# A fused attention, DeltaNet and RG-LRU layer: the order of work at the seams of its stages, and the engine of some elementwise steps

## The chip, the cores and the metric

The kernel runs on one core of one Trainium2 chip. The metric is the device time of one execution in microseconds (us). Times before: 1758.59, 1755.84 and 1751.17, median 1755.84.

## What is computed

One layer, on x of 2048 tokens by 1024 channels in float32:

```python
h = rmsnorm(x, norm_w)
u = h @ W_in                        # 1024 x 5128, split into column groups
a_q,a_k,a_v,a_z, g_q,g_k,g_v,g_z, g_b,g_a, r_x,r_z = split(u)
y_a = diff_attention(a_q, a_k, a_v, lam, subln_w) * silu(a_z)   # 4 heads, block-causal, chunk 64
y_g = gated_deltanet(...)           # causal conv of width 4 on q, k, v; chunked WY form; * silu(g_z)
y_r = rg_lru(...) * silu(r_z)       # causal conv of width 4, gates, linear scan over positions
x = x + concat(y_a, y_g, y_r) @ W_out                           # 1536 x 1024
out = rmsnorm(x, final_norm_w)
```

In diff_attention each head has two softmax maps; the second is subtracted with weight lam. The result is normalised per head.

## The kernel before

Every float32 product is made of three matmuls: each operand is split into a rounded high part and a low remainder (high by ACT, remainder by DVE), and PE adds high x high, low x high and high x low. So each weight group and each activation goes through a split before PE can use it.

**Projection stage, 0 to about 1143 us.** The tokens are taken in two halves of 1024 (hf), each of two blocks of 512 (sb). A half has 40 jobs; a job is one group of 128 columns of W_in, or, for the values, half of the 1024 contraction rows of 256 columns (`values`, two jobs that go together). `unit` (L286) does a job for one block with 24 matmuls of 128x512; `unit_v` (L297) does the values. The list `order` (L352) says which job and block come next. `half_jobs` (L1316) makes the list of jobs: the values of the first two heads, then for each GDN head its key, query, value and gate groups with four or five of the other groups (attention az, aq, ak; LRU rx, rz) between them, then what is left of the others, and last the values of the other two heads.

Weights are fetched and split by `next_w` (L1380): it waits two steps, splits the group that was fetched, and asks for the next one. At most two jobs' weights are live (`refill`, L1374); their tiles have the tag wx, of which there are five. Work that is not a matmul of a job runs in generators in the list bgs, which are advanced by `pump` between matmuls: norms and transposes of the next x block (`norm_x` L211, `next_hT` L265), the convolutions (`conv`, L349: first tap on POOL at L351, three more on DVE at L355), the triangular solve of the GDN (L576 to L649), its chain over chunks (`Gdn.main`, L674 to L709) and output (`Gdn.out`, scaling at L731), the LRU (gates L769, scan L808 and L809), and the splitting of W_out (`split_wo`, L864). The x block 2 is loaded near the end of the first half and transposed from job 39 on; block 3 is loaded after the last unit of the half.

**Attention and output projection, 1143 us to the end.** `all_scores` (L1170) yields the scores of one block of 128 queries against up to 512 keys at a time: two matmuls (L1036, L1037) into a bank with the tag tp (three bufs), a maximum on DVE (L1040), an exponential on ACT (L1048). `turn` (L1103) transposes the probabilities on PE (L1111), with evacuations on ACT (L1118) and DVE (L1120), and `apply` multiplies by the values (L1128 to L1130). `norm_sq` and `norm_out` (L1145) make the sums for the norm with two matmuls, L1148 and L1149, into the tile ss, with the tag pj (two bufs). Queries, keys, values and gates of 512 tokens come back from memory by `fetch_kv` (L996); it is called one step before it is needed. Between these, `out_stream` (L904) supplies matmuls of the output projection (L893 to L895) as filling, into the tag pj; its operands come by `load_wo` (L872, tiles lt, big, g) and `fetch_y` (L879 high, L880 low). For head 3 its result is added to the sum so far at L966, also a reader of pj.

A scheduler lays the instructions of the program on the queues of the engines and may place them earlier or later than the program has them, within their dependences; every engine then runs its own queue in order. All loads and stores go through SP's queue.

```python
pss = psum.tile([P, 256], F32, name="ss", tag="pj", bufs=2)                # L1147
...
bgs.append(next_w(2))                                                      # L1378
```

## Time and profile before

| | |
|---|---|
| times | 1758.59, 1755.84, 1751.17 us, median 1755.84 |
| the profiled execution: time, span | 1750.52 us, 1748.8 us |
| mean granted clock of PE | 0.996 |
| PE busy | 1697.3 us (97%), 9494 matmuls |
| DVE busy | 1286.4 us (74%) |
| ACT busy | 1005.7 us (58%) |
| POOL busy | 305.3 us (17%) |
| DMA | 261.65 MB, mean 150 GB/s |

The profiled execution ran 5.3 us under the median. Times inside it are counted from the start of its span. Busy PE means that a matmul is under way; its idle time is span less busy, 51.5 us. The granted clock is 1.0 at full speed.

### The profile page before, as it was taken

Reading aid. Unit: us, or ns where it says so; the run is one execution under the profiler, and the core shown is the slowest. Engines: PE = TensorE matmul, PEld = TensorE weight load, DVE = VectorE, ACT = ScalarE, POOL = GpSimd, SP = SyncE. Lnnn points to the kernel's source line nnn. Section 1 sums busy time; section 2 is a strip of 40 time slices with the busy share of each in tenths; the row PEclk is TensorE's granted clock in tenths of the full one; section 3 lists DMA queues with packets and bytes.
Section 4 is the critical chain, followed back from the end, with each engine's and each line's share of the span. In section 5 each row is a group of like instructions: output and inputs, shape, how many; then the busy total and the mean of one; then the engine's idle time right before and its main releaser. Section 6 shows DMA issues by size and latency. Waiting matters only on the chain.

```text
span 1748.8 us, 27889 instructions
## 1 busy us (share of the span) xinstructions
PE 1697.3 (97%) x9494; PEld 1414.3 (81%) x9494; DVE 1286.4 (74%) x3043; ACT 1005.7 (58%) x2568; POOL 305.3 (17%) x458
## 2 busy tenths in 40 slices
PE   7999999999999899999999999999999999999998
PEld 6887777887879888787887887977888888887786
DVE  5576786686686567678778678578787777778896
ACT  6634534535435554453553534368778878877684
POOL 3011200201101111131221210011213213211011
PEclk9999999999999999999999999999999999999999
DMA  6233242242244434435445424697797898596432
GB/s 182 68 91 94 60 121 76 82 108 68 88 121 146 145 85 133 136 115 168 137 135 173 123 88 142 185 285 197 194 245 205 273 233 232 159 285 209 162 132 103
DMA packets 309298, 261.65 MB, mean 150 GB/s; under 512 B 67082, under 2 KB 242468, under 8 KB 309156
## 3 DMA queue, kind: packets, MB, share of 16 engines
q1 hardware_dynamic: 309156, 259.87, 50.9%
q8 instruction: 75, 1.23, 0.3%
q14 instruction: 67, 0.55, 0.1%
HBM read 175.88 MB, written 83.92 MB: 149 GB/s over the span
## 4 chain that ended last, share of the span: by engine, by line
PE 61%; DVE 10%; issue 7%; DMA 4%; ACT 3%; POOL 2%; SPq 1%; POOLq 0%; DVEq 0%; ACTq 0%
PE pj L290 10%; PE pj L291 10%; PE pj L292 10%; PE pj L895 3%; PE pj L893 3%; PE pj L894 3%; PE s L1036 2%; PE s L1037 2%; PE pt L1111 2%; DVE s L355 2%; DVE tt L589 1%; DVE tt L595 1%; DMA wx<-xo_sp 1%; PE tp L542 1%; PE av L1130 1%
## 5 line engine op out<-in xcount | busy, mean ns | idle before, releaser
L290 PE MATMUL pj<-hp,wx 128*128 128x512 f32 x1120 | 461.4, 412 | 2.4 <-DVE s L367 2.4
L292 PE MATMUL pj<-hp,wx 128*128 128x512 f32 x1120 | 444.5, 397 | 0.0
L291 PE MATMUL pj<-hp,wx 128*128 128x512 f32 x1120 | 444.1, 397 | 0.0
L292 PEld LDWEIGHTS pj<-hp,wx 128*128 128x128 f32 x1120 | 210.5, 188 | 47.9
L290 PEld LDWEIGHTS pj<-hp,wx 128*128 128x128 f32 x1120 | 211.0, 188 | 45.3 <-DVE s L367 2.9
L291 PEld LDWEIGHTS pj<-hp,wx 128*128 128x128 f32 x1120 | 211.5, 189 | 41.9
L1040 DVE TENSOR_REDUCE nm<-s 128x1 f32<-128x512 f32 (+3 forms) x320 | 191.7, 605 | 28.3 <-PE s L1037 25.1
L1048 ACT ACTIVATE s<-s,nm 128x512 f32<-128x512 f32 (+3 forms) x272 | 170.8, 629 | 52.3 <-DVE nm L1040 51.4
L355 DVE SCALAR_TENSOR_TENSOR s<-raw,pcol,s 128x512 f32<-128x512 f32 x192 | 143.8, 749 | 41.7 <-POOL s L351 38.8
L279 ACT ACTIVATE wx<-wx 128x1024 fp32r<-128x1024 f32 (+1 forms) x76 | 80.5, 1059 | 88.5 <-PE pj L291 82.4
L1036 PE MATMUL s<-hp 128*128 128x512 f32 (+3 forms) x320 | 124.8, 390 | 5.0 <-ACT s L1048 3.8
L283 DVE TENSOR_TENSOR wx<-wx 128x1024 fp32r<-128x1024 f32 (+1 forms) x77 | 94.2, 1224 | 45.6 <-ACT wx L279 43.7
L1037 PE MATMUL s<-hp 128*128 128x512 f32 (+3 forms) x320 | 118.0, 369 | 0.0
L1111 PE MATMUL pt<-ident,s 128*128 128x128 f32 x544 | 86.3, 274 | 4.0 <-DVE s L1099 3.9
L589 DVE TENSOR_TENSOR tt<-lt,tt 128x248 f32<-128x248 f32 (+30 forms) x248 | 82.2, 331 | 6.2
L893 PE MATMUL pj<-g,wx 128*128 128x512 f32 x208 | 85.4, 411 | 0.1
L1099 DVE SCALAR_TENSOR_TENSOR s<-s,cf,s 128x512 f32<-128x512 f32 (+2 forms) x112 | 75.1, 701 | 11.1 <-ACT s L1087 6.5
L346 POOL COPY halo<-raw 128x3 f32<-128x3 f32 x48 | 14.9, 311 | 386.2 <-ACT raw L344 375.0
L895 PE MATMUL pj<-g,wx 128*128 128x512 f32 x208 | 82.2, 395 | 0.0
L894 PE MATMUL pj<-g,wx 128*128 128x512 f32 x208 | 82.1, 395 | 0.0
L595 DVE TENSOR_TENSOR tt<-tt 128x248 f32<-128x248 f32 (+30 forms) x248 | 76.9, 310 | 6.6
L309 PE MATMUL pj<-wx,hp 128*128 128x264 f32 (+1 forms) x256 | 77.1, 302 | 4.4 <-ACT wx L279 1.9
(337 smaller groups left out, 3849.6 us busy)
## 6 DMA issues: line engine op xcount, KB each, us to landing
wx<-in_w_in_dram SPq DMA_DIRECT2D x78, 512.0 KB, 4.2
wx<-y_sp SPq DMA_DIRECT2D x64, 512.0 KB, 6.5
hp<-k_sp SPq DMA_DIRECT2D x64, 256.0 KB, 6.5
wo_sp<-s SPq DMA_DIRECT2D x48, 256.0 KB, 2.3
v_sp<-s SPq DMA_DIRECT2D x64, 128.0 KB, 3.2
q_sp<-s SPq DMA_DIRECT2D x32, 256.0 KB, 2.3
k_sp<-s SPq DMA_DIRECT2D x32, 256.0 KB, 2.6
y_sp<-go SPq DMA_DIRECT2D x32, 256.0 KB, 2.7
```

What stands on the lines that cost most here:

```text
L290: nc.tensor.matmul(ps, wh[:, kt, :], hb[kt][:, 0, :], start=(kt == 0), stop=False)
L291: nc.tensor.matmul(ps, wh[:, kt, :], hb[kt][:, 1, :], start=False, stop=False)
L292: nc.tensor.matmul(ps, wl[:, kt, :], hb[kt][:, 0, :], start=False, stop=(kt == KT - 1))
L355: nc.vector.scalar_tensor_tensor(y, raw[:, t : t + SB], pc(wcol(t)), y, op0=ALU.mult, op1=ALU.add)
L893: nc.tensor.matmul(ps, yh, wh, start=first, stop=False)
L894: nc.tensor.matmul(ps, yh, wl, start=False, stop=False)
L895: nc.tensor.matmul(ps, yl, wh, start=False, stop=last)
L1036: nc.tensor.matmul(ps[:, :n], qq, kh[:, :n], start=True, stop=False)
L1037: nc.tensor.matmul(ps[:, :n], qq, kl[:, :n], start=False, stop=True)
L1040: nc.vector.tensor_reduce(nm[:, u, m, kb : kb + 1], ps[:, :n], axis=AX.X, op=ALU.max, negate=True)
L1048: nc.scalar.activation(ee[:, :n], ps[:, :n], AF.Exp, bias=nm[:, u, m, kb : kb + 1], accum_out=zp[:, u, m, kb : kb + 1],)
L1111: nc.tensor.transpose(pt[:, off + (u - us[0]) * P : off + (u - us[0] + 1) * P], e[(u, kt // 4)][:, (kt % 4) * P : (kt % 4 + 1) * P], ident,)
```

## The change

- `norm_x`: the scalings of the x tiles of blocks 2 and 3 (8 in all) go from POOL to ACT.
- `conv`: the first of four taps (64 in all) goes from POOL to ACT.
- `Gdn.out`: the scaling of the outputs (64 of 128x128) goes from POOL to ACT.
- `split_wo`: the subtraction (24) goes from POOL to DVE.
- `norm_out`: for head 3, the tile ss has the tag tp instead of pj.
- `all_scores`: the first two blocks of queries, keys and values are fetched at once at the start, and the second is not fetched again.
- `next_half`, in place of two calls of `next_h`: x block 3 is loaded as soon as block 2 is transposed.
- The last five of the other groups come as rx, az, rz, aq, ak instead of az, rx, aq, ak, rz, and behind the second pair of value jobs, not ahead of it. Each half ends with aq and ak, block by block.
- The weights of the second value job of the second half are fetched one job ahead, into the tile lt. For two jobs of each half, `next_w` waits no steps instead of two.

```diff
--- before.py
+++ after.py
@@ -207,6 +207,10 @@
         for t, xx in enumerate(xt):
             if sb == 1 and t < 2:
                 nc.vector.tensor_scalar(xx, xx, rs[:, t : t + 1], None, op0=ALU.mult)
+            elif sb == 3 and t < 2:
+                nc.scalar.activation(xx, xx, AF.Copy, scale=rs[:, t : t + 1])
+            elif sb > 1:
+                nc.scalar.activation(xx, xx, AF.Copy, scale=rs[:, t : t + 1])
             else:
                 nc.gpsimd.tensor_scalar(
                     xx, xx, rs[:, t : t + 1], 0.0, op0=ALU.mult, op1=ALU.add
@@ -346,10 +350,10 @@
             nc.gpsimd.tensor_copy(halo[:, gi, :], raw[:, SB : SB + 3])
         return raw
 
-    def conv(raw, wcol, bias=0.0):
+    def conv(raw, wcol, bias=None):
         y = at([P, SB], "s16", 16)
-        nc.gpsimd.tensor_scalar(
-            y, raw[:, 3 : 3 + SB], pc(wcol(3)), bias, op0=ALU.mult, op1=ALU.add
+        nc.scalar.activation(
+            y, raw[:, 3 : 3 + SB], AF.Identity, scale=pc(wcol(3)), bias=zero if bias is None else bias
         )
         for t in range(3):
             nc.vector.scalar_tensor_tensor(
@@ -728,8 +732,8 @@
                 ro, ro, 1.0 / math.sqrt(P), rn[:, 1, sl], op0=ALU.mult, op1=ALU.mult
             )
             for c in range(4):
-                nc.gpsimd.tensor_scalar(
-                    os_[:, c, :], os_[:, c, :], ro[:, c : c + 1], 0.0, op0=ALU.mult, op1=ALU.add
+                nc.scalar.activation(
+                    os_[:, c, :], os_[:, c, :], AF.Copy, scale=ro[:, c : c + 1]
                 )
             yield from wait(7)
             pt = tp()
@@ -861,7 +865,7 @@
         wp = at([P, SB], "s16", 16, F32R)
         nc.scalar.activation(wp, wr, AF.Copy)
         wl = at([P, SB], "s16", 16, F32R)
-        nc.gpsimd.tensor_tensor(wl, wr, wp.bitcast(F32), op=ALU.subtract)
+        nc.vector.tensor_tensor(wl, wr, wp.bitcast(F32), op=ALU.subtract)
         yield from wait(6)
         nc.sync.dma_start(wo_sp[e, dh, :, 0, :], wp.bitcast(F32))
         nc.sync.dma_start(wo_sp[e, dh, :, 1, :], wl.bitcast(F32))
@@ -1144,7 +1148,7 @@
 
     def norm_out(h, i, oo):
         o2, t1, oh, ol = oo
-        pss = psum.tile([P, 256], F32, name="ss", tag="pj", bufs=2)
+        pss = psum.tile([P, 256], F32, name="ss", tag="pj" if h < 3 else "tp", bufs=2 if h < 3 else 3)
         nc.tensor.matmul(pss, onesr, oh, start=True, stop=False)
         nc.tensor.matmul(pss, onesr, ol, start=False, stop=True)
         nc.scalar.activation(o2, pss, AF.Ln, scale=1.0 / P, bias=epsA)
@@ -1171,10 +1175,11 @@
         for n, (h, i) in enumerate(steps):
             if n + 1 < len(steps):
                 h2, i2 = steps[n + 1]
-                if i2 % 2 == 0 and i2 > 0:
+                if i2 % 2 == 0 and i2 > 0 and i2 // 2 not in heads[h2].q:
                     fetch_kv(heads[h2], h2, i2 // 2)
             if n == 0:
-                fetch_kv(heads[0], 0, 0)
+                for kb in range(2):
+                    fetch_kv(heads[0], 0, kb)
                 yield
             for _ in scores(heads[h], h, i, es[n]):
                 yield
@@ -1276,9 +1281,15 @@
 
     bgs.append(start_h())
 
-    def next_h(n, xt):
-        yield from next_hT(hbs[n], xt)
-        ready[n] = True
+    def next_half(xt):
+        yield from next_hT(hbs[2], xt)
+        ready[2] = True
+        yield
+        xt = load_x(3)
+        while hbs[3] is None:
+            yield
+        yield from next_hT(hbs[3], xt)
+        ready[3] = True
 
     def params():
         pps = psum.tile([P, SB], F32, name="pps", tag="tp", bufs=3)
@@ -1327,6 +1338,9 @@
                 (partial(fetch_w, COL_RZ + h * P), None, r.outp),
             ]
 
+        az, rx, aq, ak, rz = others[-5:]
+        others[-5:] = [rx, az, rz, aq, ak]
+
         def values(pair):
             return [
                 (partial(fetch_v, pair, part, pair == 0), None, (gbs if pair == 0 else None, pair))
@@ -1344,7 +1358,7 @@
             ]
             for _ in range((4, 5, 5, 4)[h]):
                 jobs.append(others.pop(0))
-        return gbs, jobs + others + values(1)
+        return gbs, jobs + values(1) + others
 
     halves = [half_jobs(hf) for hf in range(2)]
     njob = len(halves[0][1])
@@ -1363,6 +1377,7 @@
                 order += [(a, 0), (a, 1), (a + 1, 0), (a + 1, 1)]
 
     nxt = Stage()
+    ahead = {}
     nxt.j, nxt.wr, nxt.live, nxt.busy = 4, jobs[4][0](), 2, False
 
     def drop(j):
@@ -1375,13 +1390,19 @@
         if nxt.live < 2 and not nxt.busy and nxt.j < len(jobs):
             nxt.busy = True
             nxt.live += 1
-            bgs.append(next_w(2))
+
+            bgs.append(next_w(0 if nxt.j % njob in (1, njob - 3) else 2))
 
     def next_w(n):
         yield from wait(n)
         ws[nxt.j] = split_w(nxt.wr)
         nxt.j += 1
-        nxt.wr = jobs[nxt.j][0]() if nxt.j < len(jobs) else None
+        nxt.wr = ahead.pop(nxt.j, None)
+        if nxt.wr is None and nxt.j < len(jobs):
+            nxt.wr = jobs[nxt.j][0]()
+        if nxt.j == njob:
+
+            ahead[njob + 1] = fetch_v(0, 1, True, ("lt", 1))
         nxt.busy = False
         refill()
 
@@ -1413,7 +1434,7 @@
             xt2 = load_x(2)
         if hf == 0 and (j, sb) == (njob - 1, 0):
             hbs[2] = h_tiles()
-            bgs.append(next_h(2, xt2))
+            bgs.append(next_half(xt2))
         if (j, sb) == (2 * njob - 2, 0):
             next(ost)
         if (j, sb) == (2 * njob - 1, 0):
@@ -1423,7 +1444,6 @@
             advance(4)
         if (j, sb) == (njob - 1, 1):
             hbs[3] = h_tiles()
-            bgs.append(next_h(3, load_x(3)))
     while bgs:
         pump()
```

The lines of the kernel after are higher by 4 from L211 on (L893 to L897, L1036 to L1040, L629 to L633 and so on); the numbers in this document without another word are those before.

What the change moves is seen in the order of the instructions on the queues. SP's queue at the stage seam, before: q_sp, k_sp, v_sp and z_sp are the attention's operands, y_sp the output projection's (L880 loads the low part), wo_sp its weights.

```order
L1008 DMA hp<-k_sp 64x2x512 x2
L1014 DMA hp<-v_sp 128x1024
L1016 DMA sz<-z_sp 128x512
L331 DMA v_sp<-s_11534 128x2x128 x2
L331 DMA v_sp<-s_11535 128x2x128 x2
L880 DMA wx<-y_sp 128x8x128
L872 DMA g_11682<-wo_sp 128x1024
L331 DMA v_sp<-s_11647 128x2x128 x2
L331 DMA v_sp<-s_11648 128x2x128 x2
L374 DMA y_sp<-go 128x512
L375 DMA y_sp<-go 128x512
L872 DMA g_11684<-wo_sp 128x1024
```

And after (L1004 to L1020 are `fetch_kv`, L884 the low part of y, L876 the weights):

```order
L1004 DMA hp<-q_sp 64x2x512 x2
L1012 DMA hp<-k_sp 64x2x512 x4
L1018 DMA hp<-v_sp 128x1024
L1020 DMA sz<-z_sp 128x512
L848 DMA q_sp<-s_11599 128x512
L849 DMA q_sp<-s_11601 128x512
L884 DMA wx<-y_sp 128x8x128
L848 DMA k_sp<-s_11664 128x512
L849 DMA k_sp<-s_11666 128x512
L378 DMA y_sp<-go 128x512
L379 DMA y_sp<-go 128x512
L876 DMA g_11695<-wo_sp 128x1024
```

The operands of the second block, which stood behind y and the three weight loads (they begin two rows below the part shown), now stand directly behind those of the first and ahead of y.

PE's queue at the same place, before: the scores (L1036, L1037) and the first output tile (L893 to L895, whose operands are lt, big and g in turn).

```order
L893 MATMUL pj<-lt,wx 128x512
L1036 MATMUL s<-hp 128x512
L1037 MATMUL s<-hp 128x512
L894 MATMUL pj<-lt,wx 128x512
L895 MATMUL pj<-lt,wx 128x512
L893 MATMUL pj<-big,wx 128x512
L894 MATMUL pj<-big,wx 128x512
L895 MATMUL pj<-big,wx 128x512
L893 MATMUL pj<-big,wx 128x512
L894 MATMUL pj<-big,wx 128x512
L895 MATMUL pj<-big,wx 128x512
L893 MATMUL pj<-g_11678,wx 128x512
```

And after, where L1040 and L1041 are the scores, L897 and L898 the first two of the output tile's 24 matmuls, L1115 a transposition, L1132 to L1134 the product with the values:

```order
L897 MATMUL pj<-lt,wx 128x512
L1040 MATMUL s<-hp 128x512
L1041 MATMUL s<-hp 128x512
L898 MATMUL pj<-lt,wx 128x512
L1115 MATMUL pt<-ident,s_11630 128x128 x2
L1040 MATMUL s<-hp 128x512
L1041 MATMUL s<-hp 128x512
L1132 MATMUL av<-go,hp 128x256
L1040 MATMUL s<-hp 128x512
L1041 MATMUL s<-hp 128x512
L1133 MATMUL av<-go,hp 128x256
L1134 MATMUL av<-go,hp 128x256
```

The third, L899, stands 35 rows below L898, after 11 more pairs of scores and the transposes and products between them.

DVE's queue in the first GDN head of the second half, before: L612 transposes what a DMA has brought, L808 and L809 are the LRU's, L841 the low part of a query or key group, L283 a weight split, L629 a copy that PE waits for.

```order
L612 STREAM_TRANSPOSE xi<-g_6772 32x8x32 x3
L808 TENSOR_TENSOR big<-big,bg_6969 128x1024
L809 SCALAR_TENSOR_TENSOR bg_6969<-big,hlast 128x1024
L283 TENSOR_TENSOR wx<-wx 128x1024
L841 SCALAR_TENSOR_TENSOR s_7228<-pj,s_7226 128x512
L629 COPY zs<-tp 32x256 x2
L638 TENSOR_SCALAR g_6772<-tp 32x8x32 x2
```

And after:

```order
L868 TENSOR_TENSOR s_7218<-s_7139,s_7216 128x512
L812 TENSOR_TENSOR big<-big,bg_6969 128x1024
L616 STREAM_TRANSPOSE xi<-g_6772 32x8x32 x2
L813 SCALAR_TENSOR_TENSOR bg_6969<-big,hlast 128x1024
L616 STREAM_TRANSPOSE xi<-g_6772 32x8x32
L845 SCALAR_TENSOR_TENSOR s_7228<-pj,s_7226 128x512
L287 TENSOR_TENSOR wx<-wx 128x1024
L633 COPY zs<-tp 32x256 x2
L642 TENSOR_SCALAR g_6772<-tp 32x8x32 x2
```

L808 (now L812) goes ahead of the three L612 (now L616), and a subtraction of `split_wo` (L868) is new on the queue.

## Rows read from the trace of the kernel before

**Rows 1.** Windows by stage: us, PE, PEld, DVE, ACT, POOL busy (x), PEclk, DMA share, GB/s.

```profile
550.00:620.00 70.00, 65.41 (x503) 61.33 (x502) 38.28 (x112) 39.29 (x101) 12.05 (x18) 1.00 0.51 151
620.00:1135.00 515.00, 508.70 (x2775) 415.74 (x2774) 381.22 (x871) 237.66 (x577) 95.78 (x145) 1.00 0.45 135
1135.00:1200.00 65.00, 58.84 (x316) 47.98 (x316) 47.90 (x135) 47.67 (x131) 10.61 (x15) 0.92 0.94 259
...
1560.00:1748.80 188.80, 174.43 (x949) 144.31 (x947) 152.37 (x363) 132.95 (x368) 24.61 (x31) 0.99 0.50 168
1160.00:1170.00 10.00, 8.34 (x28) 6.65 (x28) 6.74 (x25) 6.20 (x22) 1.51 (x3) 0.66 1.11 255
```

**Rows 2.** Waits of PE, whole span: line and its releaser, us in total, times, longest.

```profile
PE ss L1148 <- DVE wx L966: 3.5, 5, 1.7
...
PE tp L634 <- DVE zs L629: 2.2, 1, 2.2
PE ch L682 <- DVE ct L676: 2.2, 6, 0.8
...
PE tp L787 <- DVE gw L769: 1.3, 2, 1.1
...
PE s L1036 <- DMA hp<-k_sp: 1.1, 1, 1.1
```

**Rows 3.** Timeline of PE at the half seam: start, us, instruction, idle before it.

```profile
584.14 0.39 PE L309 MATMUL pj<-wx,hp 128*128 128x264 f32 x1 [1.86 <-ACT wx L279]
...
585.43 0.39 PE L311 MATMUL pj<-wx,hp 128*128 128x264 f32 x1 [0.54 <-DVE wx L283]
...
592.74 0.55 PE L269 MATMUL tp<-ident,big 128*128 128x128 f32 x3 [0.41 <-POOL big L211]
```

**Rows 4.** Timeline of SP's queue there, the weights of the second value job.

```profile
578.09 0.38 SPq L124 DMA_DIRECT2D wx<-in_w_in_dram  x1
```

**Rows 5.** Timeline of SP's queue at the stage seam.

```profile
1139.73 0.55 SPq L880 DMA_DIRECT2D wx<-y_sp  x1
...
1148.71 2.55 SPq L1008 DMA_DIRECT2D hp<-k_sp  x4
```

**Rows 6.** Timeline of PE at the stage seam.

```profile
1145.08 0.39 PE L895 MATMUL pj<-lt,wx 128*128 128x512 f32 x1
1145.31 0.39 PE L893 MATMUL pj<-big,wx 128*128 128x512 f32 x1
...
1161.06 0.79 PE L1036 MATMUL s<-hp 128*128 128x512 f32 x1 [0.99 <-ACT s L1048]
...
1163.88 0.80 PE L1036 MATMUL s<-hp 128*128 128x512 f32 x1 [0.66 <-ACT s L1048]
```

**Rows 7.** The page's costliest groups: line, count, busy us, mean ns, idle before.

```profile
L1048 ACT ACTIVATE s<-s,nm 128x512 f32<-128x512 f32 (+3 forms) x272 | 170.8, 629 | 52.3 <-DVE nm L1040 51.4
L355 DVE SCALAR_TENSOR_TENSOR s<-raw,pcol,s 128x512 f32<-128x512 f32 x192 | 143.8, 749 | 41.7 <-POOL s L351 38.8
```

**Rows 8.** Groups of instructions by line, shapes apart, in the columns of group 7.

```profile
L473 ACT ACTIVATE s<-tp,nk 128x128 f32<-128x128 f32 x64 | 18.1, 366 | 8.5 <-PE tp L469 8.5
...
L795 ACT ACTIVATE big<-s,nsp 128x512 f32<-128x512 f32 x16 | 13.1, 816 | 0.5
...
L757 DVE TENSOR_TENSOR s<-s,s 128x512 fp32r<-128x512 f32 x16 | 11.0, 688 | 3.6 <-ACT s L755 3.5
```

**Rows 9.** Timeline of DVE around 713 us.

```profile
713.09 1.37 DVE L612 STREAM_TRANSPOSE xi<-g 32x256 f32<-32x256 f32 x3 [3.32 <-DMA g<-ts]
714.49 1.23 DVE L808 TENSOR_TENSOR big<-big,bg 128x1024 f32<-128x1024 f32 x1
```

**Rows 10.** Timeline of DVE around 820 us.

```profile
819.45 0.20 DVE L589 TENSOR_TENSOR tt<-lt,tt 128x40 f32<-128x40 f32 x1
...
820.40 1.28 DVE L589 TENSOR_TENSOR tt<-lt,tt 128x32 f32<-128x32 f32 x1
```

**Rows 11.** Timeline of POOL around 820 us.

```profile
820.31 1.33 POOL L864 TENSOR_TENSOR s<-s,s 128x512 fp32r<-128x512 f32 x1 [0.95 <-ACT s L862]
```

## The prediction

> **What bounds the kernel now.** I read the busy shares first, then the windows by stage, then who waits for whom on PE, and last the timelines at the two seams. PE is busy for 1697.3 of 1748.8 us, 97%; no other engine is above 74%. Its matmuls are the same before and after, in number and shape, so what can be won is PE's idle time, 51.5 us in all, and the time it runs at the lower clock. By stage [rows 1] the idle time is 70.00 - 65.41 = 4.6 us around the seam of the two halves, 515.00 - 508.70 = 6.3 in the rest of the second half, 65.00 - 58.84 = 6.2 at the seam to attention, 188.80 - 174.43 = 14.4 from 1560 on; the remaining 20 lie mostly at the very start, which the change leaves alone. The seam to attention also has a granted clock of 0.92: 65 x 0.08 = 5.2 us lost if PE is the bound there. In its worst ten microseconds the clock is 0.66, so 10 x 0.34 = 3.4 of the 5.2 lie there.
>
> Which waits make up the idle time is read from PE's waits [rows 2]: each term below is one of them.
>
> **The change, part by part.**
>
> *Half seam.* PE reaches the first value job of the second half and waits 1.86 us for the high part of its weights and 0.54 for the low part [rows 3]. Those weights were requested at 578.09 [rows 4] and had to land and be split on ACT and DVE before 584. With the fetch a job ahead into the tile lt, and with split and fetch no longer two pump steps late, both go: 2.4 us. The x tiles of block 3 were requested late too, between stores of values, and their scaling on POOL keeps the transposes 0.41 us [rows 3]. The block is now loaded straight after block 2, while two column groups of aq and ak run, and scaled on ACT; that wait and some 0.2 more of the same kind go. The evacuation waits there (L329) stay. Term: **-3.0 us**. Cover for the earlier loads: half a megabyte each in a stretch in which the DMA share is 0.51 [rows 1]. Without that cover the wait comes back as a wait on the x tiles, and the term falls to about -1.
>
> *Stage seam.* On SP the second key block was fetched after yl and the three g tiles (first key load of it at 1148.71, behind yl at 1139.73) [rows 5]; now it goes ahead of yl. On PE the 24 matmuls of the first output tile (L893 to L895) ran between the first scores; then the scores came one after the other and waited for ACT, 0.99 and 0.66 us [rows 6]; before these, 1.1 went to the late key block [rows 2]. Removed: 1.1 + 1.65 = 2.8 of idle, the clock's 3.4 and the rest of its 5.2, that is 1.8: 8.0 us at the most. Added: PE's order now has 12 score pairs nearly back to back, the one between L893 and L894 included, before L895 of the first output tile is reached. At full clock a pair takes 2 x 0.23 = 0.46 on PE (1145.08 to 1145.31 is one matmul) [rows 6]. ACT's exponential takes 0.629 on average [rows 7], so the least loss is 12 x (0.63 - 0.46) = 2.0. The largest is read from the trace: 1161.06 to 1163.88 are three pairs, 0.94 each [rows 6], which gives 12 x 0.48 = 5.8. I take the middle, 4.0. Term: -8.0 + 4.0 = **-4.0 us**, with -6.0 and -2.2 as its ends so long as yl is there when L895 needs it.
>
> *Tail.* For head 3 the sums of norm_out get a bank from the scores' three instead of the two of the output tiles. The five waits of L1148 for the addition L966, 3.5 us [rows 2], go. L966 still ends when it did, and the next output tile needs the same bank; the scores lose a bank for a moment. I count half: **-1.75 us**, with 0 and -3.5 as ends.
>
> *GpSimd's work, and the value jobs before the last groups.* The first tap of 64 convolutions goes to ACT. The nearest row with a scale and a bias column and the same shape is L795, 0.816 [rows 8]: 64 x 0.816 = 52 us. The 64 output scalings cost 0.366 each (L473) [rows 8]: 23 us. The 8 scalings of x, at most twice L795 each, are 13. ACT gets 88 us more in 1140, where it is busy 39.29 + 237.66 = 277 of 585 us [rows 1], 47%; it goes to 55%. DVE waits 38.8 us for POOL's tap now [rows 7] and gets most of that back, since ACT does the tap right behind the raw copy that it makes itself. PE gains little of it: each column group has a buffer of one group, 24 x 0.23 = 5.6 us. What PE does gain are three waits for DVE [rows 2]. In one, L629 stood behind L808, which ran after L612 had idled 3.32 us for a DMA [rows 9]; by the new order the 1.23 us of L808 go into that idle time: -1.2. L769 and L676 stand one or two instructions of 0.7 earlier in places where PE waits: -0.9 of 1.3 and -0.6 of 2.2. Against this I set +1.2: of the 16 bursts of four scalings on ACT (4 x 0.366 = 1.5 us each) about one holds up an evacuation that PE waits for. Term: **-1.5 us**, with -2.7 and +8 (rival D) as ends.
>
> The 24 subtractions of split_wo, now on DVE, cost 0.688 each [rows 8], 16.5 us in the second half, where DVE is busy 381.22 of 515 us [rows 1]. For what they free: a DVE instruction of 32 columns took 1.28 us beside one of them, and one of 40 columns 0.20 without [rows 10, 11]. If each of the 24 stretches one DVE instruction so, 24 x 1.08 = 26 us come back and DVE is lighter by 9; if none does, it is heavier by 16.5. PE hides either, so the sum holds it at nothing. The Trainium skill (SBUF — State Buffer, Who interferes with whom) says that a DVE instruction with two SBUF inputs contends with a GpSimd instruction that reads SBUF. The trace agrees at this place, with 1.28 against 0.20. By that rule the DVE gets lighter, the +1.2 above falls away and the sum would be -11.4 instead of -10.2.
>
> **Sum.** -3.0 - 4.0 - 1.75 - 1.5 = -10.2 us. The profiled execution took 1750.5 and would take 1740.3. It stands 5.3 us below the median of the runs, 1755.84, so against the median I forecast **1745.6 us**, 0.6% faster. About 0.5%, 8.8 us, is what a measurement can tell from no change: faster means under 1747.1, slower over 1764.6.
>
> **The rivals.**
>
> *A. The gain at the attention seam comes to nothing*: the scores run ahead, wait for ACT at 0.94 a pair, and the clock dips as before; projection gives nothing either. -3.0 - 1.75 = -4.75 remain: 1751. For it: ACT has been behind the scores here already [rows 6].
>
> *B. The clock falls during the new run of scores.* In 1160 to 1170, where PE paused about a microsecond between scores, the granted clock went to 0.66, part of the time at the lower of its two levels, 1.2 GHz [rows 1, 6]. Twelve pairs at that level cost 24 x 0.23 = 5.5 more: -10.2 + 5.5 = -4.7, 1751. Against it: attention runs like this for hundreds of microseconds at a granted clock of 0.99 from 1560 on [rows 1], with scores bound by ACT. The Trainium skill (TensorE: Matmul & The Clock Gate, A second HAM failure mode: psum-queue depth-cycling) says that a PE which pauses briefly and often between groups while it cycles PSUM banks lets its clock swing between the two levels. By that rule this rival is the outcome; the trace agrees at 1160 and not after 1560.
>
> *C, slower. PE stands still at L895 for yl.* The second key block is eight loads of 256 or 512 KB, 2.3 MB, at 259 GB/s [rows 1] 8.9 us, and yl and the g tiles are now behind it. PE is in order, so all scores behind L895 wait too, and the clock falls as it did at 1160. +8.9 + 3.4 in place of -4.0: -6.2 + 12.3 = +6, 1762. It decides when yl lands more than 11 us (12 pairs at 0.94) after the first score. Against it: yl was requested at 1139.73 and used by the first L895 at 1145.08 [rows 5, 6], so some of the delay is slack.
>
> *D. ACT becomes the engine that the projections wait for.* If each of the 16 bursts costs 0.5 us of PE, that is 8 instead of 1.2, the three order gains go with it: -8.75 + 8 = -0.8, 1755. Against it: ACT at 55%.
>
> *E, better.* The seam's waits all go (-8.0 + 2.0), the tail's whole 3.5 and the projections' 2.7: -15.2, 1741 or less.
>
> That the change doesn't do what it says is seen in none of its parts: PE's, SP's and DVE's orders move as told.
>
> **How the numbers follow.** Forecast 0.50 (own range 1741 to 1751), E 0.14, A 0.14, B 0.08, D 0.08, C 0.06. Of the forecast's 0.50 about 0.37 lie under 1747.1, with E 0.51; over 1764.6 lie the upper half of C and the tail of D beyond its price, 0.06; the rest, 0.43, is within 0.5%. The range takes in E, A, B and D: 1737 to 1757.
>
> **What would show it.** Right: no wait on the weights or on x at the half seam; the waits of L1036 on the key block gone and the clock of the 65 us at the seam above 0.95; no wait of the sums on L966; L629's wait near 1. Wrong: a wait of L895 (now L899) on y_sp of over 5 us; PE waiting for ACT's evacuations in the projections for over 5 us; PE's idle time in 1135 to 1200 still 6 or more.

## The result and the profile after

The changed kernel took 1738.11 us, median of four runs (1735.31 to 1739.77), beside 1754.9 for the kernel before on the same chip: a ratio of 0.990, 95% interval 0.988 to 0.992. That is 16.8 us, or 1%, faster. 1745.6 was forecast, in a range of 1737 to 1757. The profiled executions stand at 1750.52 and 1739.05, 11.5 us apart: the one of before lay 4.4 us under its median, the one of after 0.9 over its own, and 11.5 + 4.4 + 0.9 = 16.8. What follows explains the 11.5. In rows of the changed kernel and of e2 to e9 the lines are the new ones, higher by 4 (L634 is L638); e10 and e12 have the old ones.

The page's first part, after: busy time, share of the span and instructions.

```profile
PE 1693.0 (97%) x9494; PEld 1418.2 (82%) x9494; DVE 1271.5 (73%) x3067; ACT 1082.3 (62%) x2704; POOL 178.8 (10%) x298
```

PE does the same 9494 matmuls. POOL lost 127 us of work and ACT gained 77. PE's idle time is 1737.3 - 1693.0 = 44.3 us, 7.2 less than the 51.5 before; the other 4.3 of the 11.5 us came out of time in which PE counts as busy (1697.3 before). In the profile matmuls overlap (in [rows 6] one of 0.39 us is followed by the next after 0.23), so a short wait between two of them shows in no idle time.

Windows by stage, after (columns as in [rows 1]; the last row is looked at further down):

```profile
550.00:620.00 70.00, 68.00 (x424) 58.94 (x424) 36.22 (x93) 50.00 (x110) 0.38 (x2) 1.00 0.46 140
620.00:1135.00 515.00, 509.62 (x2813) 420.94 (x2812) 375.29 (x914) 272.27 (x645) 20.26 (x60) 1.00 0.45 136
1135.00:1200.00 65.00, 60.54 (x318) 48.90 (x318) 54.67 (x139) 57.06 (x158) 11.48 (x14) 0.97 0.87 240
1140.00:1150.00 10.00, 8.11 (x34) 5.99 (x34) 7.96 (x24) 8.12 (x25) 0.17 (x1) 0.83 1.07 328
1560.00:1737.30 177.30, 163.03 (x873) 133.85 (x873) 140.76 (x336) 124.15 (x343) 22.96 (x29) 0.99 0.47 155
510.00:520.00 10.00, 8.06 (x96) 7.28 (x95) 8.36 (x13) 4.12 (x6) 0.19 (x1) 0.71 0.75 212
```

Idle PE is 70.00 - 68.00 = 2.0 us at the half seam (4.6 in [rows 1]), 5.4 in the rest of the second half (6.3), 4.5 at the attention seam (6.2), 14.3 in the tail (14.4). But windows of the same times hold different work in two kernels whose jobs come in another order. So I also counted progress: from the timelines, the start of the 212th, 1690th, 2535th and 3802nd of the 4224 matmuls of the projections (5, 40, 60 and 90%), of the 81st and 241st scores (L1036) and the end. These numbers fall on the same work in every kernel, except that the half seam and the job order lie inside the stretch from 40 to 60%, and the last jobs inside "seam" (90% to the 81st scores). Each column is the length of a stretch in us ("start" is up to 5%), for all kernels of this study; before and after are the first two rows.

| kernel | start | to 40% | to 60% | to 90% | seam | attention | tail | span | ratio to before |
|---|---|---|---|---|---|---|---|---|---|
| before | 58.2 | 423.4 | 192.9 | 373.5 | 215.6 | 276.2 | 209.1 | 1748.8 |  |
| after | 58.2 | 417.3 | 195.4 | 368.4 | 212.4 | 276.2 | 209.4 | 1737.3 | 0.990 (0.988 to 0.992) |
| e1: all of POOL's work back | 59.7 | 423.7 | 197.6 | 375.4 | 213.2 | 276.1 | 213.1 | 1758.8 | 1.001 (1.000 to 1.002) |
| e2: second key block late | 57.6 | 417.3 | 195.1 | 368.4 | 220.2 | 276.2 | 208.8 | 1743.7 | 0.993 (0.991 to 0.995) |
| e3: sums in pj | 58.9 | 417.2 | 194.1 | 368.5 | 212.4 | 276.3 | 212.6 | 1739.9 | 0.992 (0.990 to 0.994) |
| e4: three half-seam edits undone | 58.0 | 417.2 | 193.8 | 369.0 | 210.0 | 276.2 | 207.8 | 1732.0 | 0.987 (0.985 to 0.990) |
| e5: tap on POOL | 59.5 | 423.5 | 197.3 | 369.3 | 214.2 | 276.5 | 209.9 | 1750.2 | 0.996 (0.995 to 0.998) |
| e6: subtraction on POOL | 59.5 | 417.3 | 194.2 | 372.4 | 211.9 | 276.1 | 210.6 | 1742.1 | 0.992 (0.990 to 0.994) |
| e7: output scaling on POOL | 58.7 | 417.2 | 193.9 | 368.4 | 211.2 | 276.2 | 208.4 | 1733.9 | 0.990 (0.987 to 0.992) |
| e8: job order undone | 57.4 | 417.3 | 191.3 | 368.4 | 209.4 | 276.1 | 209.8 | 1729.7 | 0.986 (0.983 to 0.988) |
| e9: az ahead of rx | 60.1 | 417.2 | 200.2 | 368.4 | 220.9 | 276.1 | 209.1 | 1752.1 | 0.998 (0.997 to 0.999) |
| e10: before, tap on ACT | 58.2 | 417.2 | 194.3 | 371.9 | 214.9 | 276.1 | 211.0 | 1743.6 | 0.993 (0.992 to 0.994) |
| e11: e8 and e7 | 59.3 | 417.2 | 189.2 | 368.4 | 208.6 | 276.3 | 212.4 | 1731.4 | 0.985 (0.983 to 0.986) |
| e12: before, tap on DVE | 58.5 | 417.1 | 193.5 | 372.8 | 214.5 | 276.2 | 211.6 | 1744.2 | 0.995 (0.993 to 0.996) |

From 5% to 40% and from 60% to 90% of the projections the change gained 6.1 and 5.1 us; in the stretch with the half seam it lost 2.5 (the granted clock from 510 to 525 us is 0.77, and 1.00 before: 3.4 us); at the attention seam it gained 3.2; in the tail nothing. "Start" spreads by 2.7 us and "tail" by 5 among kernels whose code is the same there: differences below that mean nothing in these two columns. "To 40%", "to 90%" and "attention" repeat within 0.6 us where the code is the same (attention: 276.1 to 276.5 in all fourteen). "To 60%" does not: the changed kernel and e3 have the same instructions in the same order on every queue up to 1568 us, and take 195.4 and 194.1 there. The granted clock from 510 to 525 us is 0.77 in the one and 0.89 in the other: the stretch at the lower clock lasted longer. So 1.3 us in this column can be the clock alone, and single effects of that size are not settled by it.

The waits of PE, after (whole span):

```profile
PE pj L897 <- DVE wx L970: 3.1, 3, 1.4
...
PE tp L629 <- DVE xi L616: 1.9, 2, 1.2
...
PE ch L686 <- DVE ct L680: 0.3, 1, 0.3
...
PE tp L638 <- DVE zs L633: 0.2, 1, 0.2
```

L638 <- L633 is the wait that was L634 <- L629 in [rows 2], 0.2 now and 2.2 there; L686 <- L680 was L682 <- L676, 0.3 and 2.2; that of L787 for L769 is in the list no more. New are L897 <- L970 in the tail, in place of L1148's wait, and L629 <- L616, which was L625 <- L612.

The half seam, PE's timeline after:

```profile
585.57 0.39 PE L313 MATMUL pj<-wx,hp 128*128 128x264 f32 x1 [0.56 <-ACT gb L333]
...
589.28 0.44 PE L273 MATMUL tp<-ident,big 128*128 128x128 f32 x2 [0.25 <-ACT big L211]
```

The waits for the weights, 1.86 and 0.54 in [rows 3], are gone, and POOL's 0.41 has become ACT's 0.25.

### The profile page after: what moved, and what is told of

It reads as the page before. It is cut to its first block, busy times and chain, and to the rows that moved or that the text cites. A ratio compares the mean times of both kernels' runs of the same rounds, so it can differ in the third digit from the quotient of the medians.

```text
span 1737.3 us, 27880 instructions
## 1 busy us (share of the span) xinstructions
PE 1693.0 (97%) x9494; PEld 1418.2 (82%) x9494; DVE 1271.5 (73%) x3067; ACT 1082.3 (62%) x2704; POOL 178.8 (10%) x298
## 4 chain that ended last, share of the span: by engine, by line
PE 76%; issue 7%; DVE 6%; ACT 5%; DMA 4%; POOL 2%; SPq 0%; DVEq 0%; POOLq 0%; ACTq 0%
PE pj L294 14%; PE pj L295 14%; PE pj L296 14%; PE pj L899 4%; PE pj L897 3%; PE pj L898 3%; PE s L1040 2%; PE s L1041 2%; PE pt L1115 2%; PE tp L546 2%; PE pj L313 1%; PE pj L315 1%; PE av L1132 1%; PE av L1133 1%; PE av L1134 1%
## 5 line engine op out<-in xcount | busy, mean ns | idle before, releaser
L296 PEld LDWEIGHTS pj<-hp,wx 128*128 128x128 f32 x1120 | 210.6, 188 | 48.2
L294 PEld LDWEIGHTS pj<-hp,wx 128*128 128x128 f32 x1120 | 211.1, 189 | 44.4 <-DVE s L371 1.7
L295 PEld LDWEIGHTS pj<-hp,wx 128*128 128x128 f32 x1120 | 211.6, 189 | 41.3
L1044 DVE TENSOR_REDUCE nm<-s 128x1 f32<-128x512 f32 (+3 forms) x320 | 191.3, 604 | 26.6 <-PE s L1041 23.6
L359 DVE SCALAR_TENSOR_TENSOR s<-raw,pcol,s 128x512 f32<-128x512 f32 x192 | 143.6, 748 | 29.0 <-ACT s L355 21.2
L283 ACT ACTIVATE wx<-wx 128x1024 fp32r<-128x1024 f32 (+1 forms) x75 | 79.5, 1060 | 88.6 <-PE pj L295 79.5
L1040 PE MATMUL s<-hp 128*128 128x512 f32 (+3 forms) x320 | 124.1, 388 | 4.9 <-ACT s L1052 4.1
L1041 PE MATMUL s<-hp 128*128 128x512 f32 (+3 forms) x320 | 117.1, 366 | 0.0
L1115 PE MATMUL pt<-ident,s 128*128 128x128 f32 x544 | 86.0, 274 | 3.5 <-DVE s L1103 3.4
L897 PE MATMUL pj<-g,wx 128*128 128x512 f32 x208 | 85.6, 412 | 0.0
L899 PE MATMUL pj<-g,wx 128*128 128x512 f32 x208 | 82.2, 395 | 0.0
L898 PE MATMUL pj<-g,wx 128*128 128x512 f32 x208 | 82.2, 395 | 0.0
L1040 PEld LDWEIGHTS s<-hp 128*128 128x128 f32 x320 | 60.7, 190 | 20.1 <-ACT s L1052 11.0
L1124 DVE TENSOR_TENSOR go<-pt,go 128x512 fp32r<-128x512 f32 (+1 forms) x96 | 64.2, 669 | 17.0 <-ACT go L1122 16.3
L593 DVE TENSOR_TENSOR tt<-lt,tt 128x248 f32<-128x248 f32 (+30 forms) x248 | 71.9, 290 | 5.9
```

The costliest lines, as they stand in the source:

```text
L294: nc.tensor.matmul(ps, wh[:, kt, :], hb[kt][:, 0, :], start=(kt == 0), stop=False)
L295: nc.tensor.matmul(ps, wh[:, kt, :], hb[kt][:, 1, :], start=False, stop=False)
L296: nc.tensor.matmul(ps, wl[:, kt, :], hb[kt][:, 0, :], start=False, stop=(kt == KT - 1))
L359: nc.vector.scalar_tensor_tensor(y, raw[:, t : t + SB], pc(wcol(t)), y, op0=ALU.mult, op1=ALU.add)
L897: nc.tensor.matmul(ps, yh, wh, start=first, stop=False)
L898: nc.tensor.matmul(ps, yh, wl, start=False, stop=False)
```

## The experiments

**The first four** undo one part of the change each. My theory then was that each seam had its own gain and that the moved work was worth little.

```diff
# e1: conv, Gdn.out, split_wo and norm_x as before
+        nc.gpsimd.tensor_scalar(
+            y, raw[:, 3 : 3 + SB], pc(wcol(3)), bias, op0=ALU.mult, op1=ALU.add
+        )
...
# e2
-                for kb in range(2):
-                    fetch_kv(heads[0], 0, kb)
+                fetch_kv(heads[0], 0, 0)
# e3
+        pss = psum.tile([P, 256], F32, name="ss", tag="pj", bufs=2)
# e4: job order, next_half and the value weights as before
-        others[-5:] = [rx, az, rz, aq, ak]
-        return gbs, jobs + values(1) + others
+        return gbs, jobs + others + values(1)
...
```

> The changed kernel with all of GpSimd's former work given back to it (first convolution tap, scaling of the outputs, scalings of x, subtraction of split_wo). Theory (each seam has its own gain; the moved work is worth about 2 us, in the second half's projections only): span 2 us above the changed kernel's 1737.3, about 1739 to 1740, half seam and attention seam keep their -3 and -6. Rival 1 (the moved work carries the gain, since DVE no longer waits for POOL's tap): the span goes back by 5 us or more, to 1742 to 1749, and the seams lose theirs.

Measured: 1759.93 beside 1758.46 for the kernel before, ratio 1.001. All of the gain is gone, and the theory with it. The rival had the direction, but the span of 1758.8 lies 10 us above its range; 5.2 of the 21.5 us are in the two columns that spread. The attention seam did not lose its gain, against the rival (213.2); the stretches 5 to 40% and 60 to 90% went back to 423.7 and 375.4.

> The changed kernel with the second key block fetched one step before its use again. Theory (fetching both blocks together makes the attention seam's gain of 6 us): the span is 4 to 7 us above the changed kernel's 1737.3, the wait for hp<-k_sp of 1 us and the dip of the clock near 1160 come back. Rival 2 (the seam's gain comes from the job order, which takes the value stores off SP's queue at the end): under 2 us above.

Measured: span 1743.7, 6.4 above (ratio 0.993; the intervals of this and of the changed kernel overlap). The theory holds in the trace. PE's timeline of this kernel at the seam:

```profile
1135.29 0.30 PE L1040 MATMUL s<-hp 128*128 128x128 f32 x1 [1.24 <-DMA hp<-k_sp]
...
1154.83 0.30 PE L1040 MATMUL s<-hp 128*128 128x128 f32 x1 [0.85 <-DMA hp<-k_sp]
```

The wait for the key block is there twice, 2.1 us in all, and the seam's stretch takes 220.2 instead of 212.4. The clock's dip came too: 0.91 granted in 1150 to 1170 and in 1170 to 1190, 1.00 in the changed kernel, whose own dip is the one of 0.83 in 1140 to 1150. Of the 7.8 us, about 1.7 are another such stretch ahead of the seam (0.91 in 1070 to 1090, 1.00 in the changed kernel), so about 6.1 are the key blocks'.

> The changed kernel with the sums of head 3 in the bank of the output tiles again. Theory (the wait only moved from L1148 to the first matmul of the next output tile): the span within 1 us of the changed kernel's 1737.3; PE waits 3 to 3.5 us for L966 at L1148 (now L1152) again and no longer 3.1 at L897. Rival (the bank was worth what was forecast): 1.75 us more.

Measured: span 1739.9, and 0.992 of before, where the changed kernel has 0.990; the intervals overlap. The wait goes back to L1152, and is longer than forecast:

```profile
PE ss L1152 <- DVE wx L970: 5.4, 4, 3.3
```

The tail took 212.6 us against 209.4. But the tails of ten kernels with the bank tp run from 207.8 to 213.1 (mean 209.9), and of four with pj from 209.1 to 212.6 (mean 211.1): about 1 us in the mean, which the spread doesn't settle.

> The changed kernel with the three edits at the half seam undone: the job order, the value weights a job ahead, both x blocks by one generator. Theory (3 to 3.7 us at the half seam come from these; the attention seam's 6 us from the key blocks): the half seam's waits of 1.9 and 0.5 us for weights are back, span 1740 to 1741.5, the attention seam keeps at least 4 of its 6. Rival 2 (the job order makes the attention seam's gain): span 1745 to 1747.

Measured: 1736.23, ratio 0.987, span 1732.0, 5.3 us under the changed kernel's; the intervals of the two ratios overlap, so the times alone don't tell them apart. Neither theory had the sign. By the stretches the half seam's edits as a whole cost time: the one to the 81st scores takes 210.0 without them and 212.4 with them, the one to 60% 193.8 and 195.4, near what the clock alone can make there.

**Which part of the moved work, and which of the three edits?**

```diff
# e5: only conv's first tap back on POOL; e6: only the subtraction of split_wo
+        nc.gpsimd.tensor_tensor(wl, wr, wp.bitcast(F32), op=ALU.subtract)
# e7: only the scaling in Gdn.out
+                nc.gpsimd.tensor_scalar(
+                    os_[:, c, :], os_[:, c, :], ro[:, c : c + 1], 0.0, op0=ALU.mult, op1=ALU.add
+                )
# e8: only the job order
-        az, rx, aq, ak, rz = others[-5:]
-        others[-5:] = [rx, az, rz, aq, ak]
-        return gbs, jobs + values(1) + others
+        return gbs, jobs + others + values(1)
```

> The changed kernel with only the first convolution tap back on GpSimd. Theory now (VectorE runs in order; where it stood at the second tap until GpSimd's first was done, the chain of the DeltaNet behind it came late, and PE with it): most of what giving all the work back cost returns: the waits of L682 for L676 (2 us in 6) come back, and the progress of the projections at 60% to 90% of their matmuls is 4 to 7 us behind the changed kernel; VectorE's idle time before the second tap is near 39 us again. Rival (the shared port: GpSimd's subtraction of split_wo and the scalings stretch VectorE's instructions): under 2 us behind.

Measured: span 1750.2, ratio 0.996. The stretch to 40% is 423.5 again, as in the kernel before (the changed one: 417.3); the later stretches lose 1.9, 0.9 and 1.8. PE's waits from 60 to 480 us in this kernel:

```profile
PE ch L686 <- DVE ct L680: 2.1, 6, 0.8
...
PE ch L700 <- DVE ct L694: 0.6, 1, 0.6
```

and in the changed one:

```profile
PE pj L294 <- DVE s L371: 1.4, 1, 1.4
```

The mechanism is seen on DVE in this kernel, around 202 us, and on PE behind it:

```profile
201.62 0.75 DVE L359 SCALAR_TENSOR_TENSOR s<-raw,pcol,s 128x512 f32<-128x512 f32 x1 [0.75 <-POOL s L355]
...
204.91 0.69 DVE L371 SCALAR_TENSOR_TENSOR s<-s,s 128x512 f32<-128x512 f32 x1
205.57 0.69 DVE L377 TENSOR_TENSOR go<-go 128x512 fp32r<-128x512 f32 x1
206.18 0.35 DVE L680 SCALAR_TENSOR_TENSOR ct<-ch,ngam,s 128x128 f32<-128x128 f32 x1
```

```profile
206.58 0.49 PE L686 MATMUL ch<-ct,g 128*128 128x128 f32 x2 [0.77 <-DVE ct L680]
```

DVE stands 0.75 us for POOL's tap; all that is queued behind it comes later, at the end L680, and PE stands 0.77 us for that. In the changed kernel DVE doesn't wait there, and L680 also goes ahead of L377:

```profile
201.41 0.69 DVE L371 SCALAR_TENSOR_TENSOR s<-s,s 128x512 f32<-128x512 f32 x1
202.02 0.35 DVE L680 SCALAR_TENSOR_TENSOR ct<-ch,ngam,s 128x128 f32<-128x128 f32 x1
202.28 0.68 DVE L377 TENSOR_TENSOR go<-go 128x512 fp32r<-128x512 f32 x1
```

Part of that is the order, which the scheduler makes. The page's group of the second to fourth taps, in this kernel and in the changed one, shows the idle time before them:

```profile
L359 DVE SCALAR_TENSOR_TENSOR s<-raw,pcol,s 128x512 f32<-128x512 f32 x192 | 143.5, 747 | 46.4 <-POOL s L355 44.2
```

```profile
L359 DVE SCALAR_TENSOR_TENSOR s<-raw,pcol,s 128x512 f32<-128x512 f32 x192 | 143.6, 748 | 29.0 <-ACT s L355 21.2
```

DVE still stands 21.2 us for the tap when ACT does it. So the sum of DVE's waits is not what PE loses: what counts is which of them have something behind them that PE needs.

> The changed kernel with only the 24 subtractions of split_wo back on GpSimd. Theory (the tap): nothing before 620 us, and under 2 us in the second half. Rival (the shared port): VectorE loses about 12 us in 13 instructions beside the subtraction, and 3 to 5 us come back on PE between 660 and 1010 us.

Measured: span 1742.1, ratio 0.992 (the interval overlaps the changed kernel's). The stretch 60 to 90% takes 372.4 instead of 368.4; the stretch to 40% doesn't move, since these subtractions are in the second half only. So 4.0 us come back, as the rival had it, with a loss on DVE near the size named: the two groups of the solve on DVE, in this kernel and in the changed one,

```profile
L593 DVE TENSOR_TENSOR tt<-lt,tt 128x248 f32<-128x248 f32 (+30 forms) x248 | 78.5, 316 | 6.1
L599 DVE TENSOR_TENSOR tt<-tt 128x248 f32<-128x248 f32 (+30 forms) x248 | 75.2, 303 | 6.2
```

```profile
L593 DVE TENSOR_TENSOR tt<-lt,tt 128x248 f32<-128x248 f32 (+30 forms) x248 | 71.9, 290 | 5.9
L599 DVE TENSOR_TENSOR tt<-tt 128x248 f32<-128x248 f32 (+30 forms) x248 | 71.9, 290 | 5.7
```

lose 9.9 us beside POOL (78.5 + 75.2 against 71.9 + 71.9). The order moved too: L812 goes behind the three L616 again, and L633, which PE waits for, starts 1.3 us later (715.60 and 714.31). On PE the new wait is one of 1.47 us for L633 at 716 (0.22 in the changed kernel), and behind it comes a stretch at the lower clock: 0.83 granted from 710 to 730 us, 1.00 in the changed kernel, or 3.4 of the 4.0 us. In the kernel before, a wait of 2.22 us at the same place was followed by no such stretch. How much is the contention, how much the order and how much the clock alone, this run doesn't tell apart. That the subtraction costs something is borne out by all kernels together: the stretch 60 to 90% takes 371.9 to 375.4 us in the five that have it on POOL and 368.4 to 369.3 in the nine that have it on DVE.

> The changed kernel with only the scaling of the DeltaNet's outputs back on GpSimd. Theory (the tap): within 1 us of the changed kernel in both halves; ACT loses 23 us of work and PE gains nothing of it. Rival (the bursts on ACT hold up evacuations): 1 to 2 us faster.

Measured: span 1733.9, 3.4 under the changed kernel, of which 1.5 are at the half seam's stretch and 1.2 at the attention seam (ratio 0.990, not told apart from the changed kernel's). In the stretches without a seam nothing moved (417.2 and 368.4), as the theory had it. Where something did, the clock can make it: in 510 to 525 us it is 0.89 here and 0.77 in the changed kernel (e3, with the scaling on ACT, has 0.89 and takes 194.1 against 193.9 here), and in 1130 to 1150 it is 1.00 here and 0.91 there. So a gain of the scaling on GpSimd is not shown.

> The changed kernel with only the order of the last jobs undone; the value weights a job ahead and both x blocks by one generator stay. Theory (the order of the jobs costs about 4 to 5 us beside the last solves of both halves, the other two edits give the 3 us at the half seam): span 1729 to 1732, below the 1732.0 of the kernel with all three undone; no wait of the solve (L629, now L633 side) and of the second value weights near 511 us. Rival (the early loads are what disturbs, not the order): span 1737 as the changed kernel.

Measured: 1731.12, ratio **0.986** (0.983 to 0.988), span 1729.7. Its interval only touches the changed kernel's, so the times point the same way. The theory holds: the job order alone costs 195.4 - 191.3 = 4.1 us at the half seam (2.8 by the 194.1 of e3) and 212.4 - 209.4 = 3.0 in the stretch to the 81st scores. These 3.0 lie at the end of the second half, ahead of the seam itself: PE's waits from 1030 to 1120 us come to 2.3 us in the changed kernel, and there are none here. The other two edits, compared with e4, are worth 193.8 - 191.3 = 2.5 at the half seam.

Where the job order costs it, in the changed kernel: DVE, then PE, around 511 us.

```profile
509.00 0.43 DVE L616 STREAM_TRANSPOSE xi<-g 32x256 f32<-32x256 f32 x1 [0.48 <-DMA g<-ts]
509.37 2.30 DVE L813 TENSOR_TENSOR_SCAN bg<-big,zero 128x1024 f32<-128x1024 f32 x1
511.69 0.90 DVE L616 STREAM_TRANSPOSE xi<-g 32x256 f32<-32x256 f32 x2
...
513.23 1.22 DVE L287 TENSOR_TENSOR wx<-wx 128x1024 fp32r<-128x1024 f32 x1
```

```profile
510.87 0.28 PE L314 MATMUL pj<-wx,hp 128*128 128x256 f32 x1
510.99 0.28 PE L315 MATMUL pj<-wx,hp 128*128 128x256 f32 x1
...
512.65 0.69 PE L629 MATMUL tp<-xi,g 32*32 32x32 f32 x30 [1.20 <-DVE xi L616]
...
514.51 0.58 PE L315 MATMUL pj<-wx,hp 128*128 128x256 f32 x1 [0.73 <-DVE wx L287]
...
515.53 0.41 PE L313 MATMUL pj<-wx,hp 128*128 128x256 f32 x1
515.74 0.41 PE L314 MATMUL pj<-wx,hp 128*128 128x256 f32 x1
```

With rx one job earlier, the scan of the last LRU head (L813, 2.30 us) comes between the transposes L616 of the last DeltaNet head's solve. PE waits 1.20 us for these and then 0.73 for the weights of the value job that now stands here. Behind the two waits a matmul of the value job follows the last one after 0.21 us, where it was 0.12: the granted clock of this stretch is 0.71 (last of the windows above). Of the 4.1 us about 3.4 are this lower clock (15 us at 0.77 in place of 1.00). With the job order undone it is

```profile
510.00:520.00 10.00, 10.00 (x116) 7.47 (x116) 5.95 (x11) 6.36 (x8) 0.30 (x1) 1.00 0.62 161
```

The Trainium skill (TensorE: Matmul & The Clock Gate, A second HAM failure mode: psum-queue depth-cycling) says that a PE which cycles through PSUM banks and pauses briefly between groups of matmuls, often enough, lets its clock swing. The trace agrees so far as two pauses of 1.20 and 0.73 us, 1.1 us apart, were followed by the lower level. It does not where two pauses of 1.86 and 0.54 us at the half seam before ([rows 3]) were followed by none: the clock from 580 to 590 us there is 1.00.

**Is it the scan, or the value jobs themselves?**

```diff
# e9
-        others[-5:] = [rx, az, rz, aq, ak]
+        others[-5:] = [az, rx, rz, aq, ak]
```

> The changed kernel with az ahead of rx among the last five groups (az, rx, rz, aq, ak): the input of the last LRU head comes one job later, and its scan of 2.3 us (L809, now L813) lies behind the solve's transposes L616 on VectorE, not among them; the value jobs stay ahead of aq and ak. Theory (the job order's cost is the scan that stands in front of L616, PE's wait of 1.2 us for it, 0.7 for the weights and the lower clock behind them): span 3 to 5 us under the changed kernel's 1737.3, granted clock of 1.0 from 510 to 520 us. Rival (value jobs beside the last solve cost this by themselves): within 1 us of 1737.3.

Measured: 1754.91, ratio 0.998, span 1752.1: neither, and 14.8 us above the changed kernel, of which 4.8 are at the half seam and 8.5 in the stretch to the 81st scores. The clock from 510 to 520 is 1.00, as the theory had it, but the scan now stands in front of the next thing that PE needs:

```profile
519.31 2.34 DVE L813 TENSOR_TENSOR_SCAN bg<-big,zero 128x1024 f32<-128x1024 f32 x1
521.58 0.32 DVE L694 TENSOR_SCALAR ct<-ch,cd 128x128 f32<-128x128 f32 x1
```

```profile
519.65 0.38 PE L686 MATMUL ch<-s,g 128*128 128x128 f32 x2
521.95 0.49 PE L700 MATMUL ch<-ct,s 128*128 128x128 f32 x2 [1.91 <-DVE ct L694]
```

PE waits 1.91 us for the chain's L694 behind a scan of 2.34, and 1.93 at the end of the second half, again behind the scan (1091.91). PE also waits longer at the half seam (1.8 us for an x tile, 1.7 for L333), and that stretch takes 200.2. The rest of the 8.5 us stays open.

The scan's place on DVE is not the whole cause, though. With the job order undone (e8) it stands in front of L694 just the same, DVE first and PE below:

```profile
521.34 2.33 DVE L813 TENSOR_TENSOR_SCAN bg<-big,zero 128x1024 f32<-128x1024 f32 x1
523.60 0.32 DVE L694 TENSOR_SCALAR ct<-ch,cd 128x128 f32<-128x128 f32 x1
```

```profile
522.58 0.38 PE L686 MATMUL ch<-s,g 128*128 128x128 f32 x2
...
524.20 0.38 PE L700 MATMUL ch<-ct,s 128*128 128x128 f32 x2
```

PE doesn't wait. From the scan's start to L700 its queue has eleven matmuls of 128x512 of an ordinary job, at 0.23 us each; in e9 it has two of a value job, at 0.12 us each, and none between L686 and L700. So what PE has to do meanwhile decides. The value jobs beside the last solve are part of the cost, as the rival had it in kind; by these rows the scan costs PE a wait where they stand beside it. How much of the cost is the scan's place and how much the value jobs', no run here separates.

**One part alone, on the kernel before.**

```diff
# e10
+        nc.scalar.activation(
+            y, raw[:, 3 : 3 + SB], AF.Identity, scale=pc(wcol(3)), bias=zero if bias is None else bias
+        )
# e12
-        nc.gpsimd.tensor_scalar(
+        nc.vector.tensor_scalar(
             y, raw[:, 3 : 3 + SB], pc(wcol(3)), bias, op0=ALU.mult, op1=ALU.add
         )
```

> The kernel before with one edit: the first convolution tap on ACT. Theory (the tap is most of the gain): span 7 to 11 us under 1748.8, 1738 to 1742; at 90% of the projections' matmuls 7 to 9 us ahead of the kernel before. Rival (the tap helps only with the subtractions and scalings also gone): under 4 us.

Measured: 1745.46, ratio 0.993 (0.992 to 0.994), span 1743.6. By the times that is 12.7 us under the kernel before, by the profiled executions 5.2. At 90% of the projections it is 6.3 us ahead of the kernel before, 6.2 of them from the first 40%; the tail gave 1.9 back, within that column's spread. The span's 5.2 lies between the theory's 7 and the rival's 4, the progress at 90% a little under the theory's 7 to 9: the tap alone is most of the projections' gain, not of all.

> The kernel before with the first convolution tap on VectorE itself. It tells what of the tap's move counts. If it is that VectorE no longer stands in its queue for another engine's tap, the place is gained without ACT: VectorE's 38.8 us of waiting go, 64 x 0.5 to 0.7 = 32 to 45 us of work come, each at a place where it would mostly have waited, and the span lies 3 us or more under 1748.8, 1741 to 1746, near the kernel with the tap on ACT (1743.6). If it is that the instructions behind the tap (the DeltaNet's chain) are held up as long by its work as by the wait, the span is 1747 or more, and the waits of L682 for L676 stay at 2 us.

Measured: ratio 0.995 (0.993 to 0.996), span 1744.2, as with the tap on ACT. The stretch to 40% is 417.1. The group of the other three taps, idle time last, and the tap itself:

```profile
L355 DVE SCALAR_TENSOR_TENSOR s<-raw,pcol,s 128x512 f32<-128x512 f32 x192 | 143.6, 748 | 3.5
```

```profile
L351 DVE TENSOR_SCALAR s<-raw,pcol x64: 476/492/545, 42.3 to 1065.6; 128x512 f32<-128x512 f32 x64
```

So the gain isn't ACT's: it comes when DVE no longer stands in its queue for POOL. 64 x 0.492 = 31.5 us of work on DVE took the place of 38.8 us of waiting and PE gained the same 6 us. What this run can't separate is the port: POOL also reads less beside DVE in it.

**The best of both.**

> The changed kernel with the job order undone and the scaling of the DeltaNet's outputs back on GpSimd. Theory (the two gains add: 7.6 and 2 to 3 us): span 1726 to 1728, 0.983 of the kernel before. Rival (they overlap): 1729 to 1731, as with the job order undone alone.

The edits are those of e8 and e7 together. Measured: 1731.69, ratio 0.985 (0.983 to 0.986), span 1731.4. It isn't told apart from e8 (0.986). Their ratios lie 0.4 to 0.5% under the changed kernel's 0.990. In the stretches e11 takes 2.1 us less than e8 to 60% and 0.8 less at the seam, and 1.9 and 2.6 more in the start and the tail, the two columns that spread; one execution of each doesn't settle whether the gains add.

## Why the prediction was right, and where it was wrong

The time lay in the range, near its lower end, and the direction was right, but the sum was right partly by luck: errors in its terms cancelled.

- **Projections, -1.5 forecast, about -11 measured** (6.1 + 5.1). The step that failed: "PE gains little of it: each column group has a buffer of one group". That holds for evacuations, but not for the DeltaNet's chain, in which PE needs DVE's result at once and DVE runs in order. I had the row with 38.8 us of waiting for the tap, and the waits of L682 for L676, and did not put the two together as cause and effect: 6.2 us are the tap (e5, e10). The three waits that I named went nearly whole: L629's from 2.2 to 0.2, L676's from 2.2 to 0.3, L769's from 1.3 to nothing, 5.2 us where I took 2.7 off. The remaining 6 I had not named. I took idle time as all that could be won and set the first half's aside as left alone by the change; from 60 to 480 us PE's idle time fell from 4.7 to 1.4 us, and of the 6.1 us gained up to 40% some 3 came out of time in which PE counts as busy.
- **The subtraction of split_wo: held at nothing, worth 4.0** in the second half (e6), 3.4 of them at the lower clock behind one wait of PE. "PE hides either" failed. DVE's instructions of the solve, which POOL stretched (by 9.9 us in e6), lie ahead of work that PE waits for; that the stretching made the wait, and not the order that moved with it, isn't shown. The Trainium skill's rule (SBUF — State Buffer, Who interferes with whom), which I set aside, pointed the right way.
- **Half seam, -3.0 forecast.** The edits meant there did what was forecast: both waits for weights went, and the next_half and ahead parts are worth 2.5 (e8 against e4). But I gave the job order no price, apart from naming it in a heading. It costs 4.1 there (3.4 of them the lower clock) and 3.0 at the end of the second half. What was missed could be read from the order alone: the input of the LRU one job earlier, hence the scan among the transposes, and value jobs in place of longer matmuls beside it.
- **Attention seam, -4.0 forecast, -3.2 measured**; the mechanism was right. Fetching both key blocks alone is worth about 6.1 in the changed kernel (e2: 7.8, less the 1.7 ahead of the seam), my end of -6.0, and the job order gives 3.0 back in the same column. yl did not come late: SP and PE, after,

```profile
1131.06 2.75 SPq L1012 DMA_DIRECT2D hp<-k_sp  x4
...
1139.70 0.55 SPq L884 DMA_DIRECT2D wx<-y_sp  x1
```

```profile
1146.60 0.50 PE L1040 MATMUL s<-hp 128*128 128x512 f32 x1 [0.45 <-ACT s L1052]
...
1148.41 0.38 PE L1040 MATMUL s<-hp 128*128 128x256 f32 x1 [0.61 <-ACT s L1052]
...
1152.07 0.39 PE L899 MATMUL pj<-lt,wx 128*128 128x512 f32 x1
```

yl is requested at 1139.70 (1139.73 in [rows 5]), behind the second block, which now starts at 1131.06; L899 runs at 1152.07 without a wait. Rival C falls. The longest waits of the scores for ACT there are 0.45 and 0.61 us, shorter than the 0.99 and 0.66 of [rows 6], and the clock dips less: 0.97 in 1135 to 1200 (0.92 before), 0.83 at its worst (0.66). That dip is part of rival B, at a fraction of its 5.5.
- **Tail, -1.75 forecast, 0 in the trace** (209.4 and 209.1). As feared in that step, the wait came back one place further on: 3.1 us at L897 in place of 3.5 at L1148. The bank itself may be worth 1 us (e3 and the means above), which isn't resolved: e3's tail has a stretch at the lower clock (0.96 granted in 1620 to 1660) that the changed kernel's has not.
- **Rival D** (ACT as the bound) didn't come: with the output scalings back on POOL (e7) the stretches to 40% and 60 to 90% are the same, so the 1.2 us I set against the bursts are not seen there. Rival E (1741 or less) came nearest in time, but with other terms: it had the attention seam at -6 and the tail at -3.5.

## What to carry to other kernels

In-order engines hand their waits on: an instruction that waits for a third engine delays all that is queued behind it, so price such a wait by who needs the instructions behind it, not by how busy the engine is. A long instruction (here a scan of 2.3 us) in front of a dependent chain costs a wait on the engine at the chain's other end unless that engine has enough else on its queue: the same scan cost PE 1.91 us in e9 and nothing in e8. Moving jobs moves both the long instruction and what covers it; look up in the order where they land. And undo each part of a bundle by itself: here one of nine parts cost 6 to 7 us, and without it the others gave half as much again.
